# Reciprocal row sums sent to DRAM as single words, without transposes, and their factor of one half moved into v

## The chip, the core and the metric

The kernel runs on one core of a Trainium2 chip. The core has a matrix engine (TensorE, PE in the profile), a vector engine (VectorE, DVE), an engine for functions and copies (ScalarE, ACT), a general one (GpSimd, POOL) and SyncE (SP), which here only issues DMA transfers. DMAs are also issued from the queues of ACT and POOL. The metric is the time of one execution on the device in microseconds (us); the times before are a median of 3 executions, and a separate execution was profiled.

## The reference

One decoder block over 512 tokens of width 1024, all in float32. The input is normalised and goes through one wide projection. From that come two attention branches of 8 heads of width 64 each: the first (fox) has a forget bias in its logits, the second (moba) works on blocks of keys, which for 512 tokens and blocks of 256 comes to causal attention. Each branch is multiplied by a SiLU gate and projected; the two are merged with sigmoid gates, projected once more and added to the input. What the change touches is this part of it:

```
p = softmax(logits)                       # exp / row sum
y = (p @ v) * silu(z)                     # per head, then heads side by side
```

The softmax divides by the sum over keys, one number for each head and query. The kernel computes SiLU as z * (1 + tanh(z / 2)) * 0.5, so a factor of one half goes in somewhere.

## The kernel before, in words

Matmuls of full float32 accuracy are made of three products of rounded parts: each operand is split into a high part and the rest (`hi`, `lo`), so nearly every operand passes ACT (a copy, which rounds) and DVE (a subtraction) before PE reads it.

Attention runs as four groups of four heads: fox a, fox b, moba a, moba b (`plan`). In a group the heads are taken in two pairs (`pr` 0 and 1). For a head:

- `Tr` transposes q and k of a pair.
- `Aa` computes, for four blocks of 128 queries, the logits (L571, L572), the mask and the negated maximum on DVE (L574), and the exponential on ACT (L576), which also sums each row into `rs`. Queries lie on the partitions, so the sums of a head are a column of 128 numbers for each of the 4 blocks. After the second head of a pair `inverse_sums` takes the reciprocal of the pair's 2 x 4 columns on DVE (L591) into `ri`.
- `Bb` transposes the exponentials (L616), splits them (L622, L623) and multiplies them with v (L626, L627). v is held as its high part and the rest side by side (`evac_v`, L351 on ACT and L352 on DVE), so that the result has both in two halves of the partitions, which L651 and L652 add into `ypair`. The result is transposed: the 64 columns of a head lie on partitions, the 512 queries along them.
- `Yp` multiplies `ypair` by the SiLU gate (`ZS`, made in `unit_z` with no factor of one half) and the reciprocal sums, and splits the product (L677 to L680).

For `Yp` the reciprocals must lie along the queries and be the same on all 64 partitions of a head. For seven of the eight pairs this goes through DRAM:

- `sums_out` transposes the 128 x 8 reciprocals on PE into 8 x 128 (L596), copies them out of PSUM on ACT times 0.5 (L598) and stores them from ACT's queue as 8 rows of 512 bytes into `R_dram` (L599).
- `sums_in` reads each head's 2 KB back onto 64 partitions, two broadcast loads from ACT's queue (L606), into `rinv_bc`, which has one buffer. These can be issued only when the store has landed.
- `Yp` multiplies the broadcast with the gate on POOL (L677), and the result with `ypair` on DVE (L678).

For the last pair (moba b, pair 1) nothing goes through DRAM. `Yp` spreads the reciprocals times 0.5 over 64 columns a head on POOL (L670), transposes the four 128 x 128 blocks of that on PE (L673) into a bank of PSUM, and multiplies the gate with it on DVE (L674).

Between the steps of the attention groups stand units of other work ("filler"): the projections of later groups, gate projections and the first branch projection. A projection unit (`unit`) takes one of two PSUM banks (`pj`), does 24 matmuls and is copied out by ACT or DVE. After the attention come the merge gates (`GA`, `GB`), the moba branch projection (`wm`, L695 to L697), which reads what `Yp` made, and the output projection. The last `Yp` is called three units into the first gate products.

The functions are traced in a written order, and a planner at build time then sets the order of each engine's instructions, by its own durations, among those whose inputs and buffers are ready. An engine carries out its instructions in that order, the DMA issues of its queue among them: an issue that waits for an earlier transfer holds up what is queued behind it on the same engine. Transposes and projections share three PSUM banks (`tp`).

Of the kernel before, what the change touches and what calls it, by code (L numbers as in the profile page):

```python
# [29 lines left out]
def fox_moba_kernel(ctx: ExitStack, tc, xT, x, w_in, w_fl, w_fox, w_moba, w_out, cst, rope, out):  # L30
# [28 lines left out]
    def tp(name):  # L59
        return pst("tp", 3, name)  # L60
# [285 lines left out]
    def evac_v(p, name, t):  # L346
# [4 lines left out]
        A.activation(v[:, t, :, 0:HD], pv, AF.Copy)  # L351
        V.tensor_tensor(out=v[:, t, :, HD:P], in0=pv, in1=v[:, t, :, 0:HD].bitcast(F32), op=OP.subtract)  # L352
# [163 lines left out]
    def attn_group(br, half, gq, gk):  # L516
# [72 lines left out]
        def inverse_sums(pr):  # L589
            h0 = hb + 2 * pr  # L590
            V.reciprocal(ri[:, h0:h0 + 2, :], rs[:, h0:h0 + 2, :])  # L591

        def sums_out(pr):
            h0 = hb + 2 * pr
            p = tp("p_ri")
            T.transpose(p[:8, :P], ri[:, h0:h0 + 2, :].rearrange("p h t -> p (h t)"), ident)  # L596
            rt = sb.tile([8, P], F32, name="rinv_t", tag="rinv_t", bufs=1)
            A.activation(rt, p[:8, :P], AF.Copy, scale=0.5)  # L598
            A.dma_start(out=R_dram[h0:h0 + 2].rearrange("h t p -> (h t) p"), in_=rt)  # L599

        def sums_in(pr):
            if last and pr:
                return
            rb = st["r", pr] = stage["pool"].tile([P, S], F32, name="rinv_bc", tag="rinv_bc", bufs=1)
# [4 lines left out]
        def Bb(h):  # L609
            def go():  # L610
# [42 lines left out]
                if o == 0 and not (last and pr):  # L653
                    sums_out(pr)
                elif pr:
                    sums_in(1)
            return go

        def Yp(pr):
            def go():  # L660
# [4 lines left out]
                if last and pr:  # L665
                    zr, rb = ZS[br, gp], pst("lg", 2, "p_rinv")
                    h0 = hb + 2 * pr
                    rw = t2("u", 4, "rinv_w")
                    for o in range(2):
                        G.tensor_scalar(rw.rearrange("p (t o d) -> p t o d", o=2, d=HD)[:, :, o, :],  # L670
                                        ri[:, h0 + o, :, None].to_broadcast([P, NT, HD]), 0.5, None, op0=OP.mult)
                    for t in range(NT):
                        T.transpose(rb[:, t * P:(t + 1) * P], rw[:, t * P:(t + 1) * P], ident)  # L673
                    V.tensor_tensor(out=zr, in0=zr, in1=rb, op=OP.mult)  # L674
                else:
                    zr = st["r", pr]
                    G.tensor_tensor(out=zr, in0=ZS[br, gp], in1=zr, op=OP.mult)  # L677
# [558 lines left out]
```

## Time and profile before

| What | us |
|---|---|
| Median of 3 executions | 425.06 |
| Lowest and highest of them | 424.13, 425.23 |
| The profiled execution | 424.43 |
| Its span, first to last instruction | 422.5 |
| PE busy | 417.3 |
| VectorE (DVE) busy | 327.5 |
| ScalarE (ACT) busy | 279.7 |
| GpSimd (POOL) busy | 102.4 |

A row of the profile names the line of the kernel, the engine, the operation, what is written and read, and the shape, then how often (x) and how long. L596 is line 596. An engine's name with a q behind it (ACTq) is its queue: DMA issues and waits on semaphores, which aren't counted as busy time. PEld is the loading of weights into the array, which runs beside the matmuls. Matmuls overlap in the array, so one that lasts 0.27 us can take up less of PE's time; the chain of work in order of time shows what each adds to the path. "idle before <-releaser" behind a row is how long its engine stood idle before it and what ended that. The span is some 2 us shorter than the time of the same execution.

### The profile page before, as it was taken

To read this page: it belongs to the slowest core of one execution; us is meant where nothing else is said; L and a number is where in the kernel's file an instruction comes from. 1 tells how busy PE (TensorE), PEld (TensorE's weight loads), DVE (VectorE), ACT (ScalarE), POOL (GpSimd) and SP (SyncE) were. 2 spreads that over 40 slices of the span, in tenths; PEclk is the share of its full clock that TensorE was granted. 3 is DMA by queue.
4 is the path that set the end of the run, shared out by engine and by line. 5 is a ranking of instruction groups with operands and counts; after the bars stand their busy time and mean duration, and the time that the engine had idled before them with its cause. 6 is when DMAs were issued, how large, how long until landed. Compare 5 with 4: busy or idle time off the path is not lost.

```text
span 422.5 us, 7680 instructions
## 1 busy us (share of the span) xinstructions
PE 417.3 (99%) x2912; PEld 388.0 (92%) x2912; DVE 327.5 (78%) x575; ACT 279.7 (66%) x528; POOL 102.4 (24%) x120
## 2 busy tenths in 40 slices
PE   8999999999999999999999999999999999999996
PEld 6998899999999998899998888899999989988885
DVE  4669968799968779668666778767979698689883
ACT  5987327877877978569758687756655535686450
POOL 1067600224235550025650100340000000022230
PEclk9999999999999999999999999999999999999999
DMA  7982325567252123303122311673142603697494
GB/s 227 396 290 98 99 101 159 158 192 223 63 168 102 45 83 101 102 24 101 33 93 78 102 47 27 240 247 110 35 169 67 233 2 117 213 249 119 99 138 162
DMA packets 24484, 56.10 MB, mean 133 GB/s; under 512 B 2824, under 2 KB 7616, under 8 KB 24448
## 3 DMA queue, kind: packets, MB, share of 16 engines
q1 hardware_dynamic: 13536, 38.11, 28.0%
q0 software_dynamic: 3392, 8.39, 9.0%
q10 hardware_dynamic: 7520, 9.11, 6.8%
q8 instruction: 23, 0.38, 0.4%
q14 instruction: 13, 0.11, 0.1%
HBM read 48.11 MB, written 6.32 MB: 129 GB/s over the span
## 4 chain that ended last, share of the span: by engine, by line
PE 97%; DMA 1%; SPq 0%; DVE 0%; issue 0%
PE pb_GB L769 3%; PE pb_GA L769 3%; PE pb_GA L766 3%; PE pb_GB L766 3%; PE pb_GB L768 3%; PE pb_GA L768 3%; PE po L957 3%; PE po L956 3%; PE po L955 3%; PE pv L627 2%; PE lg L572 2%; PE pv L626 2%; PE lg L571 2%; PE pf L696 2%; PE pm L697 2%; PE pf L697 2%
## 5 line engine op out<-in xcount | busy, mean ns | idle before, releaser
L342 POOL TENSOR_TENSOR ff<-ss,mh 128x8 f32<-128x8 f32 x16 | 29.7, 1857 | 72.7 <-DVE ss L340 54.2
L576 ACT ACTIVATE p<-p,negm 128x128 f32<-128x128 f32 (+1 forms) x64 | 35.7, 558 | 13.0 <-DVE negm L574 12.0
L574 DVE CUSTOM_DVE_ANT_0 p<-lg,mask 128x128 f32<-128x128 f32 (+1 forms) x64 | 30.7, 485 | 15.0 <-PE lg L572 14.5
L904 POOL DMA_DIRECT2D wr_o<-in_w_out_dram x4 | 4.9, 1293 | 95.5 <-ACT wr_o L903 95.5
L142 DVE TENSOR_TENSOR wl_GA<-wr_ga,wh_GA 128x1024 fp32r<-128x1024 f32 x14 | 16.9, 1222 | 5.9 <-ACT wh_GA L140 3.9
L140 ACT ACTIVATE wh_GA<-wr_ga 128x1024 fp32r<-128x1024 f32 x14 | 14.6, 1059 | 10.1 <-PE pb_GA L768 5.1
L140 ACT ACTIVATE wh_GB<-wr_gb 128x1024 fp32r<-128x1024 f32 x14 | 14.6, 1059 | 9.5 <-PE pm L696 3.5
L571 PE MATMUL lg<-KH,QS 128*128 128x128 f32 (+1 forms) x64 | 20.4, 328 | 0.0
L918 DVE TENSOR_TENSOR wl_o<-wr_o,wh_o 128x1024 fp32r<-128x1024 f32 x14 | 17.0, 1219 | 3.8 <-ACT wh_o L917 3.8
L917 ACT ACTIVATE wh_o<-wr_o 128x1024 fp32r<-128x1024 f32 x14 | 14.8, 1060 | 7.6 <-PE pb_GB L768 2.8
L142 DVE TENSOR_TENSOR wl_GB<-wr_gb,wh_GB 128x1024 fp32r<-128x1024 f32 x14 | 16.9, 1221 | 3.5 <-ACT wh_GB L140 3.5
L652 DVE TENSOR_TENSOR ypair<-pv,ysh 64x512 f32<-64x512 f32 x16 | 11.0, 687 | 6.2 <-ACT ysh L651 5.8
L546 DVE SCALAR_TENSOR_TENSOR KL<-p_kT,cs,KH 64x512 fp32r<-64x512 f32 x16 | 12.0, 747 | 3.4 <-ACT KH L543 3.2
L623 DVE TENSOR_TENSOR ptl<-p_a,pth 128x512 fp32r<-128x512 f32 x16 | 10.9, 684 | 4.3 <-ACT pth L622 4.2
L651 ACT ACTIVATE ysh<-pv 64x512 f32<-64x512 f32 x16 | 9.5, 593 | 7.1 <-PE pv L627 4.7
L336 DVE TENSOR_REDUCE ss<-sq 128x8 f32<-128x512 f32 x16 | 10.8, 680 | 3.6 <-ACT sq L335 3.6
L766 PE MATMUL pb_GA<-Gh,wh_GA 128*128 128x256 f32 x48 | 13.5, 282 | 0.0
L768 PE MATMUL pb_GA<-Gl,wh_GA 128*128 128x256 f32 x48 | 13.5, 281 | 0.0
L769 PE MATMUL pb_GA<-Gh,wl_GA 128*128 128x256 f32 x48 | 13.5, 281 | 0.0
L769 PE MATMUL pb_GB<-Gh,wl_GB 128*128 128x256 f32 x48 | 13.5, 281 | 0.0
L768 PE MATMUL pb_GB<-Gl,wh_GB 128*128 128x256 f32 x48 | 13.4, 281 | 0.0
L766 PE MATMUL pb_GB<-Gh,wh_GB 128*128 128x256 f32 x48 | 13.3, 281 | 0.0
(461 smaller groups left out, 1794.1 us busy)
## 6 DMA issues: line engine op xcount, KB each, us to landing
wr_ga<-in_w_in_dram SPq DMA_DIRECT2D x8, 512.0 KB
wr_gb<-in_w_in_dram SPq DMA_DIRECT2D x8, 512.0 KB
wr_o<-in_w_out_dram SPq DMA_DIRECT2D x8, 512.0 KB
xt<-in_xT_dram SPq DMA_DIRECT2D x8, 256.0 KB
x<-in_x_dram SPq DMA_DIRECT2D x8, 256.0 KB
s_dramh<-sum_sh ACTq DMA_DIRECT2D x8, 256.0 KB
s_draml<-sum_sl ACTq DMA_DIRECT2D x8, 256.0 KB
wr_wf<-in_w_fox_dram SPq DMA_DIRECT2D x4, 512.0 KB
```

Source lines behind the costliest of these rows:

```text
L140: A.activation(hi[:, :, 0:n], src, AF.Copy)
L142: eng.tensor_tensor(out=lo[:, q, 0:n], in0=src[:, q], in1=hi[:, q, 0:n].bitcast(F32), op=OP.subtract)
L342: G.tensor_tensor(out=f2, in0=ss.rearrange("p t h -> p (t h)"), in1=mh, op=OP.pow)
L571: T.matmul(lg[:, :n], qs[:, qt], kh[:, :n], start=True, stop=False)
L574: V.tensor_tensor_reduce(pt, lg[:, :n], mask[:, 512 - n:512], -0.125, 3.0e38, op0=OP.add, op1=OP.min, accum_out=mkn[:, hh, i:i + 1])
L576: A.activation(pt, pt, AF.Exp, bias=mkn[:, hh, i:i + 1], scale=-1.0, accum_out=rs[:, hh, i:i + 1])
L697: T.matmul(p, lo[:, k, cc], yh, start=False, stop=(k == 3))
L766: T.matmul(o, hi[:, k, cc], lh, start=(n < 3 and c == 0 and k == 0), stop=False, skip_group_check=True)
L768: T.matmul(o, hi[:, k, cc], ll, start=False, stop=False, skip_group_check=True)
L769: T.matmul(o, lo[:, k, cc], lh, start=False, stop=(k == 3), skip_group_check=True)
L917: A.activation(wide(hi), wide(R[key, c]), AF.Copy)
L918: V.tensor_tensor(out=wide(lo), in0=wide(R[key, c]), in1=wide(hi).bitcast(F32), op=OP.subtract)
```

## The change

Three things change.

The reciprocals are stored from where they lie. `sums_out` has no transpose and no copy any more: one DMA reads the 128 x 8 numbers of a pair from `ri` and writes them to `R_dram` in the same order as before. There the numbers of one partition lie 128 words apart.

The factor of one half goes from the copy (L598, and L670 for the last pair) to v: the ACT copy of v's high part is scaled by 0.5, and the DVE subtraction becomes a multiplication by 0.5 and a subtraction in one instruction.

The last pair goes through DRAM like the others: a store after its first head, two broadcast loads after its second, and the gate product on POOL. Its `rinv_bc` takes one of the four buffers of the tag "u", which outlives the attention stage, because its `Yp` runs in the next one.

```diff
-        A.activation(v[:, t, :, 0:HD], pv, AF.Copy)
-        V.tensor_tensor(out=v[:, t, :, HD:P], in0=pv, in1=v[:, t, :, 0:HD].bitcast(F32), op=OP.subtract)
+        A.activation(v[:, t, :, 0:HD], pv, AF.Copy, scale=0.5)
+        V.scalar_tensor_tensor(v[:, t, :, HD:P], pv, 0.5, v[:, t, :, 0:HD].bitcast(F32), op0=OP.mult, op1=OP.subtract)
...
         def inverse_sums(pr):
-            h0 = hb + 2 * pr
-            V.reciprocal(ri[:, h0:h0 + 2, :], rs[:, h0:h0 + 2, :])
+            h = slice(hb + 2 * pr, hb + 2 * pr + 2)
+            V.reciprocal(ri[:, h, :], rs[:, h, :])
 
         def sums_out(pr):
-            h0 = hb + 2 * pr
-            p = tp("p_ri")
-            T.transpose(p[:8, :P], ri[:, h0:h0 + 2, :].rearrange("p h t -> p (h t)"), ident)
-            rt = sb.tile([8, P], F32, name="rinv_t", tag="rinv_t", bufs=1)
-            A.activation(rt, p[:8, :P], AF.Copy, scale=0.5)
-            A.dma_start(out=R_dram[h0:h0 + 2].rearrange("h t p -> (h t) p"), in_=rt)
+            h = slice(hb + 2 * pr, hb + 2 * pr + 2)
+            A.dma_start(out=R_dram[h].rearrange("h t p -> p h t"), in_=ri[:, h, :])
 
         def sums_in(pr):
-            if last and pr:
-                return
-            rb = st["r", pr] = stage["pool"].tile([P, S], F32, name="rinv_bc", tag="rinv_bc", bufs=1)
+            rb = st["r", pr] = (t2("u", 4, "rinv_bc") if last and pr else
+                                stage["pool"].tile([P, S], F32, name="rinv_bc", tag="rinv_bc", bufs=1))
...
-                if o == 0 and not (last and pr):
+                if o == 0:
                     sums_out(pr)
                 elif pr:
                     sums_in(1)
...
-                if last and pr:
-                    zr, rb = ZS[br, gp], pst("lg", 2, "p_rinv")
-                    h0 = hb + 2 * pr
-                    rw = t2("u", 4, "rinv_w")
-                    for o in range(2):
-                        G.tensor_scalar(rw.rearrange("p (t o d) -> p t o d", o=2, d=HD)[:, :, o, :],
-                                        ri[:, h0 + o, :, None].to_broadcast([P, NT, HD]), 0.5, None, op0=OP.mult)
-                    for t in range(NT):
-                        T.transpose(rb[:, t * P:(t + 1) * P], rw[:, t * P:(t + 1) * P], ident)
-                    V.tensor_tensor(out=zr, in0=zr, in1=rb, op=OP.mult)
-                else:
-                    zr = st["r", pr]
-                    G.tensor_tensor(out=zr, in0=ZS[br, gp], in1=zr, op=OP.mult)
+                zr = st["r", pr]
+                G.tensor_tensor(out=zr, in0=ZS[br, gp], in1=zr, op=OP.mult)
                 V.tensor_tensor(out=y, in0=y, in1=zr, op=OP.mult)
```

## The prediction, made before the result was known

> **What bounds the kernel now.** I read the page first: busy time by engine, granted clock, the chain of work that ended last.
>
> ```profile
> PE 417.3 (99%) x2912; PEld 388.0 (92%) x2912; DVE 327.5 (78%) x575; ACT 279.7 (66%) x528; POOL 102.4 (24%) x120
> PEclk9999999999999999999999999999999999999999
> PE 97%; DMA 1%; SPq 0%; DVE 0%; issue 0%
> ```
>
> The chain is TensorE from one end to the other, at full granted clock. An average can hide a stage in which PE waits, so next the busy time of the stretches that the change touches, the four attention groups and the first gate products (columns: PE, PEld, DVE, ACT, POOL, clock, DMA share, GB/s):
>
> ```profile
> 65.00:110.00 45.00, 45.00 (x370) 44.31 (x369) 40.31 (x90) 34.35 (x79) 12.42 (x9) 1.00 0.57 173
> 205.00:250.00 45.00, 45.00 (x295) 40.83 (x294) 31.96 (x67) 31.74 (x67) 12.47 (x14) 1.00 0.25 80
> 250.00:284.00 34.00, 34.00 (x211) 30.19 (x210) 25.90 (x46) 24.38 (x49) 8.42 (x11) 1.00 0.46 152
> 284.00:345.00 61.00, 61.00 (x485) 59.57 (x484) 50.21 (x50) 35.41 (x50) 0.00 (x0) 1.00 0.35 111
> ```
>
> PE is busy for the whole of each. So here time comes off only where PE work comes off, and it is added only where some other engine makes PE wait. Everything below is asked in those two ways.
>
> **The PE work that goes.** The chain in order of time gives each matmul its own share of the path (start, us on the path):
>
> ```profile
> 91.38 0.11 PE p_ri L596
> ...
> 256.07 0.11 PE p_ri L596
> ...
> 288.24 0.44 PE p_rinv L673 x4
> ```
> ```profile
> L596 PE MATMUL p_ri<-ident,rinv x7: 270/271/272, 91.2 to 255.9; 128*8 128x128 f32 x7
> ...
> L673 PE MATMUL p_rinv<-ident,rinv_w x4: 270/272/273, 288.1 to 288.4; 128*128 128x128 f32 x4
> ```
>
> The two p_ri rows are the first and the last of the seven. A transpose lasts 0.27 us, but they overlap in the array, and on the path each takes 0.11. The change removes 7 x 0.11 = 0.77 us and the four of the last pair, 0.44 us: together 1.21 us. Nothing is put on PE in their place.
>
> **What goes from the other engines.** ACT loses seven copies of the small result, DVE one product with PSUM, POOL the two spreads of the last pair; POOL gets an eighth gate product instead (1.29 us, the last shape of the second fence):
>
> ```profile
> L598 ACT ACTIVATE rinv_t<-p_ri x7: 247/266/267, 91.6 to 256.6; 8x128 f32<-8x128 f32 x7
> ...
> L674 DVE TENSOR_TENSOR zs_mzb<-zs_mzb,p_rinv x1: 686/686/686, 288.7 to 288.7; 128x512 f32<-128x512 f32 x1
> ...
> L670 POOL TENSOR_SCALAR rinv_w<-rinv x2: 837/1343/1849, 280.0 to 281.8; 128x256 f32<-128x256 f32 x2
> ```
> ```profile
> L677 POOL TENSOR_TENSOR rinv_bc<-zs_mzb,rinv_bc x1: 1294/1294/1294, 263.1 to 263.1; 128x512 f32<-128x512 f32 x1
> ```
>
> That is 1.9 us of ACT, 0.7 of DVE and 1.4 of POOL, all beside a full PE: worth nothing by itself. Banks of PSUM come free too, worth nothing while PE never waits.
>
> **The half in v.** The 16 copies of v get a constant factor and the 16 subtractions become a multiply and subtract in one. The nearest rows are the same two operations on the q and k halves, with and without a factor:
>
> ```profile
> L539 DVE SCALAR_TENSOR_TENSOR QS<-p_qT,cs,QS x16: 744/750/759, 67.6 to 249.9; 64x512 fp32r<-64x512 f32 x16
> ...
> L652 DVE TENSOR_TENSOR ypair<-pv,ysh x16: 673/689/697, 96.5 to 281.1; 64x512 f32<-64x512 f32 x16
> ```
> ```profile
> L538 ACT ACTIVATE QS<-p_qT,cs x16: 669/682/687, 66.5 to 249.2; 64x512 fp32r<-64x512 f32 x16
> ...
> L651 ACT ACTIVATE ysh<-pv x16: 589/592/602, 95.4 to 280.2; 64x512 f32<-64x512 f32 x16
> ```
>
> At most 61 ns more on DVE and 90 on ACT, so 16 x 0.061 = 1.0 us and 16 x 0.090 = 1.4 us at the top; at the bottom nothing, or a few ns less. The rows differ by a per-partition factor, here it is a constant, so I take the lower half. What waits for these is the PSUM bank of the next projection unit, and the windows show PE full with what ACT and DVE do now. Cost on the path zero; were the cover gone, 0.15 us for each of 16 units, 2.4 us.
>
> **The store, which is the unknown.** It now moves 2 heads x 4 blocks x 128 words straight from where the reciprocal lies. In DRAM neighbouring words of a partition are 128 words apart, so 8 rows of 512 bytes become 1024 words of 4 bytes. The store is issued from ACT's queue, and the two broadcast loads that read it back are issued there as well; they wait for it to land, and with them all ACT work queued behind. This is how it stands at the last of the seven round trips and at the one with the longest distance:
>
> ```profile
> 256.60 0.25 ACT L598 ACTIVATE rinv_t<-p_ri 8x128 f32<-8x128 f32 x1
> 256.88 0.27 ACTq L599 DMA_DIRECT2D r_dram<-rinv_t  x1
> 257.20 1.06 ACT L140 ACTIVATE wh_GA<-wr_ga 128x1024 fp32r<-128x1024 f32 x1 [0.35 <-DVE wr_ga L730]
> 258.14 0.45 ACTq L606 DMA_DIRECT2D rinv_bc<-r_dram  x1
> ...
> 230.91 0.27 ACTq L599 DMA_DIRECT2D r_dram<-rinv_t  x1
> ...
> 233.81 1.11 ACTq L606 DMA_DIRECT2D rinv_bc<-r_dram  x2
> 234.97 0.60 ACT L651 ACTIVATE ysh<-pv 64x512 f32<-64x512 f32 x1 [2.19 <-PE p_b L616]
> ```
> ```profile
> L606 ACTq EVENT_SEMAPHORE  x11: 17/38/1266, 93.5 to 257.3; - x11
> ```
>
> From store to first load is 1.26 and 2.90 us, middle 2.1; the 8-row store can land within 1.26. ACT's queue already waits up to 1266 ns ahead of a load, and ACT has stood idle 2.19 us, while the window 205 to 250 shows PE at 45.00 of 45.00. So an ACT stand of about 2.2 us is covered.
>
> How much later do 1024 words land? No row has a packet of that size, so bounds from the queues:
>
> ```profile
> q1 hardware_dynamic: 13536, 38.11, 28.0%
> ...
> q10 hardware_dynamic: 7520, 9.11, 6.8%
> ```
>
> Spread over 16 engines it is 64 packets each. Upper end: each costs as much as ACT's queue's average packet, 0.068 x 16 x 422.5 us / 7520 = 61 ns, for 1211 bytes; 64 x 61 ns = 3.9 us. Lower end: the other queue's packet is 0.28 x 16 x 422.5 / 13536 = 140 ns for 2815 bytes; the line through both is 49 ns per 1000 bytes and 2 ns at no bytes, so 64 x 2 ns = 0.1 us. I take 1 us: time goes with bytes in these rows, but they hold few small writes. The store then lands within about 1.3 + 1 = 2.3 us and the loads wait 0 to 1 us more than now, which the 2.2 us cover. Cost on the path: zero.
>
> The Trainium skill, "DMA: Bandwidth & Descriptors", section "Rules for kernel authors", speaks against this store: a non-contiguous last dimension becomes one descriptor per element, and one should rearrange so that it is contiguous; its "Specifications" add that writes under 512 B are done as read-modify-write. No run so far shows such a write. The same page's measured table ("Bandwidth") has loads of 64 small packets at about 10.5 ns a packet; as an estimate by that page 64 would be 0.7 us, and the sum would be the same as with my 1 us.
>
> Against lateness stands that the store no longer waits for its turn on PE. The reciprocal is there well before:
>
> ```profile
> 249.31 0.18 DVE L591 RECIPROCAL rinv<-rsum 128x8 f32<-128x8 f32 x1
> ```
>
> It ends at 249.5 and the transpose of it came at 256.07, the store at 256.88. The store may now be issued up to 7 us earlier, wherever the planner finds ACT's queue free.
>
> **The eighth round trip** is new: one store and two loads, 0.27 + 2 x 0.46 = 1.2 us of ACT's queue (the fence above), less than the 1.9 us of copies removed. Behind its wait on ACT stand copies for the gate products; the same 2.2 us cover holds. On POOL the product waits for the broadcast, and the page has POOL empty from 284 to 345. Its result is first read by the moba projection:
>
> ```profile
> L695 PE MATMUL pm<-yhm,wh_wm x32: 388/392/403, 331.7 to 383.6; 128*128 128x512 f32 x32
> ```
>
> That is some 40 us after it is made today (about 291), so even a round trip of 10 us is hidden. SP's queue gets nothing new.
>
> **Sum.** Against the profiled execution (424.43 us, of which 422.5 are span): 424.43 - 1.21 = 423.2. The median shown is 425.06, the profiled one lies 0.63 below it. The four executions (424.13, 424.43, 425.06, 425.23) have a mean of 424.71, and I set the change against that: 424.71 - 1.21 = 423.5 us, 0.37% under the median. About 0.3% (1.28 us, so 423.78 to 426.34) is what a measurement of this kernel can tell from no change, so a good part of this case falls inside it.
>
> **Rivals.**
> - *The words land late and ACT holds up PE* (slower). Place: ACT's queue at each load of the sums. With the upper end, 3.9 us, the store lands 5.2 us after its issue, ACT stands 5.2 - 2.1 = 3.1 us, 0.9 more than is covered, eight times: 7.2 us, so 430.7 us. It decides from 3.0 us of lateness on (1.3 + 3.0 - 2.1 = 2.2); each 0.1 us more costs 0.8. At 3.5 us it is 4.0, 427.5 us. For it: one ordered queue, and a wait of 1.27 us there already. Against it: the two queues' times go with bytes, and the store can go out earlier. The skill's rule on one descriptor per element names this danger; by the rows here it is the less likely.
> - *The gain doesn't arrive*: the place of a transpose is taken by a wait of PE for what came beside it, or the planner, which sets another order, leaves small gaps. Then 1.21 us come back as idle time and it stays at 424.7 us. For it: ACT and DVE gain up to 2.4 us of work in the v units. Against it: the chain has PE on 97%, with no engine close behind.
>
> **How the numbers follow.** The forecast, nothing new on PE's path: 0.60; its own range is 424.13 - 1.21 = 422.9 to 425.23 - 1.21 = 424.0, with a few tenths for small gaps. Most of it, 0.44, lies below 423.78, 0.16 above. Late words: 0.26, of which 0.24 slower beyond 0.3% and 0.02 within. Gain not arriving: 0.14, of which 0.12 within and 0.02 slower. Faster 0.44, same 0.30, slower 0.26. The range goes from 422.6 (0.3 below the forecast's own) to 428.0, about half of the late words: it leaves out some 0.02 below and 0.13 above.
>
> **What would show it.** Right: no p_ri and p_rinv row, PE still full from 25 to 381 us, matmuls 11 fewer, eight stores and sixteen loads, the v subtraction at 0.41 to 0.48 us, the store issued soon after the reciprocal, the wait ahead of the loads under 2.2 us. Wrong: an ACT wait on the sums of 3 us or more with PE idle beside it, a store whose issue is itself long (now 0.27 us), the DMA share rising around the stores, or PE gaps in another stage, which would mean the planner's order and not the words.

## The result and the profile after

The changed kernel takes 491.88 us (median of 6 executions, 481.71 to 494.21), the kernel before 424.69 us beside it (6 executions, 424.13 to 425.23). Between the least disturbed executions of the two (481.71 and 484.08 us for the changed kernel) the ratio is 1.137, with a 95% interval of 1.135 to 1.139, or 58 us; the profiled execution of the changed kernel, from which the account below is taken, is one of the longer ones with 491.16 us and a span of 489.5 us, so its single figures are good to some 3%. Between the medians the ratio is 1.158. The range of the prediction ended at 428.0.

Busy time by engine, PE in 40 slices, the granted clock, ACT's DMA queue and the chain of the changed kernel:

```profile
PE 434.4 (89%) x2901; PEld 401.9 (82%) x2901; DVE 327.5 (67%) x574; ACT 277.8 (57%) x521; POOL 103.3 (21%) x119
PE   8999999949699599498698699499689999999997
PEclk9999999979899889799599799799979999999999
...
q10 hardware_dynamic: 15888, 9.38, 9.0%
...
PE 62%; DMA 18%; issue 7%; DVE 5%; ACT 3%; POOL 2%; ACTq 2%; SPq 0%; DVEq 0%; POOLq 0%
DMA r_dram<-rinv 14%; DMA rinv_bc<-r_dram 3%; PE pb_GB L753 3%; PE pb_GB L750 3%; PE pb_GB L752 3%; PE po L941 3%; PE po L940 3%; PE po L939 3%; PE pb_GA L750 2%; PE pb_GA L752 2%; PE pb_GA L753 2%; ACTq L601 2%; PE pm L681 2%; PE pm L680 2%; PE pm L679 2%
```

TensorE had the chain to itself before (97%); now 14% of it, 0.141 of 489.5 = 69 us, is the store of the reciprocals. PE's row, which should read 9 throughout, has holes, and behind most of them the clock has one too. The waits of PE in the changed kernel (who waits, for whom, us in all, times, longest):

```profile
PE pj_fvb L314 <- ACT qn_fkb L321: 8.0, 1, 8.0
PE p_cc L611 <- DVE KL L546: 7.1, 1, 7.1
PE pj_mkb L314 <- ACT qn_mqb L321: 6.6, 1, 6.6
PE pv L621 <- ACT pth L617: 6.4, 1, 6.4
PE pz_mzb L413 <- DVE v_mvb L352: 6.0, 1, 6.0
PE pj_mva L314 <- ACT qn_mka L321: 5.9, 1, 5.9
PE pb_GA L750 <- ACT wh_GA L140: 5.5, 1, 5.5
PE lg L571 <- ACT KH L543: 4.3, 1, 4.3
```

Eight waits, one for each round trip, 49.8 us together. None of the releasers has anything to do with the reciprocals: they are copies of a projection, of keys, of exponentials, of gate weights. Why they came late is seen on ACT's own timeline, at one of the round trips (start, duration; brackets: idle before):

```profile
222.87 0.36 ACTq L595 DMA_DIRECT2D r_dram<-rinv  x1
...
225.39 1.06 ACT L140 ACTIVATE wh_mvb<-wr_mvb 128x1024 fp32r<-128x1024 f32 x1
233.81 1.10 ACTq L601 DMA_DIRECT2D rinv_bc<-r_dram  x2
234.96 0.68 ACT L541 ACTIVATE KH<-p_kT,cs 64x512 fp32r<-64x512 f32 x1 [8.51 <-issue]
```
```profile
L601 ACTq EVENT_SEMAPHORE  x13: 17/38/10442, 92.6 to 338.6; - x13
```

The store is issued at 222.87. ACT goes on with other work for 3.6 us, and then its queue stands until 233.81, because the loads wait for the store to land. The first load goes out 10.9 us after the store; over the eight round trips the two are 9.4 to 13.0 us apart, 11.5 in the mean. The longest wait ahead of a load is now 10442 ns, where it was 1266.

Seven of the gaps come about in this way. The eighth (pb_GA, 350.9 to 356.4) comes later than ACT's stand and by another way: the broadcast of the last pair, issued at 343.07, lets POOL go on only at 352.77, and the products that wait for it one after the other stand ahead of the next gate weights in DVE's and ACT's order:

```profile
352.77 1.26 POOL L661 TENSOR_TENSOR rinv_bc<-zs_mzb,rinv_bc 128x512 f32<-128x512 f32 x1 [14.37 <-DMA rinv_bc<-r_dram]
...
354.06 0.69 DVE L662 TENSOR_TENSOR ypair<-ypair,rinv_bc 128x512 f32<-128x512 f32 x1 [6.98 <-POOL rinv_bc L661]
...
354.78 0.63 ACT L663 ACTIVATE yhm<-ypair 128x512 fp32r<-128x512 f32 x1 [7.53 <-DVE ypair L662]
```

One of the prediction's windows, as it looks now (PE, PEld, DVE, ACT, POOL, clock, DMA share, GB/s):

```profile
205.00:250.00 45.00, 38.31 (x272) 36.97 (x273) 26.77 (x58) 27.60 (x61) 12.36 (x15) 0.85 0.19 53
```

PE is no longer full, and while it is busy it does less: in 45 us from 205 it is busy for 38.31 us and does 272 matmuls, where it did 295. The stretch after one gap, in steps of 2 us, shows the second loss:

```profile
228.00:230.00 2.00, 2.00 (x20) 1.99 (x18) 0.00 (x0) 0.00 (x0) 0.03 (x1) 1.00 0.00 0
...
234.00:236.00 2.00, 0.00 (x0) 0.00 (x0) 0.00 (x0) 1.03 (x2) 0.00 (x0) 0.50 0.45 96
...
240.00:242.00 2.00, 2.00 (x10) 1.90 (x10) 1.96 (x8) 0.99 (x4) 0.27 (x1) 0.50 0.78 262
242.00:244.00 2.00, 2.00 (x15) 1.92 (x14) 0.00 (x0) 0.38 (x1) 1.88 (x2) 0.90 0.03 8
244.00:246.00 2.00, 2.00 (x17) 1.86 (x17) 1.41 (x5) 1.37 (x4) 1.84 (x5) 1.00 0.00 0
```

PE stands for the 6.6 us of the list above, from about 230.2 to 236.8, the granted clock falls to 0.50, and it stays there until about 242.4, with PE busy again: 10 matmuls in 2 us, where 17 to 20 go through at full clock.

So the 67.0 us of longer span (489.5 - 422.5) split in two. PE's idle time grew from 422.5 - 417.3 = 5.2 to 489.5 - 434.4 = 55.1 us: 49.9 us, the eight waits. PE's busy time grew from 417.3 to 434.4 although 1.2 us of work was gone: 18.3 us. Nearly all of that is the clock: PE's busy time in each slice of 1 us, times the part of the clock that was not granted in it, adds up to 16.9 us.

### The profile page after: what moved, and what is told of

Same layout as the page of the kernel before. It is cut to its first block, busy times and chain, and to the rows that moved or that the text cites. A ratio compares the mean times of both kernels' runs of the same rounds, so it can differ in the third digit from the quotient of the medians.

```text
span 489.5 us, 7673 instructions
## 1 busy us (share of the span) xinstructions
PE 434.4 (89%) x2901; PEld 401.9 (82%) x2901; DVE 327.5 (67%) x574; ACT 277.8 (57%) x521; POOL 103.3 (21%) x119
## 3 DMA queue, kind: packets, MB, share of 16 engines
q10 hardware_dynamic: 15888, 9.38, 9.0%
## 4 chain that ended last, share of the span: by engine, by line
PE 62%; DMA 18%; issue 7%; DVE 5%; ACT 3%; POOL 2%; ACTq 2%; SPq 0%; DVEq 0%; POOLq 0%
DMA r_dram<-rinv 14%; DMA rinv_bc<-r_dram 3%; PE pb_GB L753 3%; PE pb_GB L750 3%; PE pb_GB L752 3%; PE po L941 3%; PE po L940 3%; PE po L939 3%; PE pb_GA L750 2%; PE pb_GA L752 2%; PE pb_GA L753 2%; ACTq L601 2%; PE pm L681 2%; PE pm L680 2%; PE pm L679 2%
## 5 line engine op out<-in xcount | busy, mean ns | idle before, releaser
L541 ACT ACTIVATE KH<-p_kT,cs 64x512 fp32r<-64x512 f32 x16 | 10.8, 678 | 27.9 <-issue 27.7
L142 DVE TENSOR_TENSOR wl_GA<-wr_ga,wh_GA 128x1024 fp32r<-128x1024 f32 x14 | 16.9, 1222 | 5.0 <-ACT wh_GA L140 5.0
L142 DVE TENSOR_TENSOR wl_GB<-wr_gb,wh_GB 128x1024 fp32r<-128x1024 f32 x14 | 16.9, 1223 | 3.5 <-ACT wh_GB L140 3.5
L618 DVE TENSOR_TENSOR ptl<-p_b,pth 128x512 fp32r<-128x512 f32 x16 | 10.9, 683 | 10.2 <-ACT pth L617 10.1
L314 PE MATMUL pj_fvb<-wh_fvb,Gh 128*128 128x256 f32 x32 | 10.0, 312 | 8.0 <-ACT qn_fkb L321 8.0
L617 ACT ACTIVATE pth<-p_b 128x512 fp32r<-128x512 f32 x16 | 9.5, 595 | 12.8 <-issue 10.2
L571 PEld LDWEIGHTS lg<-KH,QS 128*128 128x128 f32 x64 | 12.2, 191 | 5.1 <-ACT KH L543 4.5
L314 PE MATMUL pj_mkb<-wh_mkb,Gh 128*128 128x256 f32 x32 | 10.5, 327 | 6.6 <-ACT qn_mqb L321 6.6
L314 PE MATMUL pj_mva<-wh_mva,Gh 128*128 128x256 f32 x32 | 10.0, 313 | 5.9 <-ACT qn_mka L321 5.9
```

The source lines that it names most:

```text
L142: eng.tensor_tensor(out=lo[:, q, 0:n], in0=src[:, q], in1=hi[:, q, 0:n].bitcast(F32), op=OP.subtract)
L314: T.matmul(p[:, :n], Gh[:, kk, st], hi[:, k, :n], start=(kk == 0), stop=False)
L571: T.matmul(lg[:, :n], qs[:, qt], kh[:, :n], start=True, stop=False)
```

## The experiments

The theory after the result: a store of 1024 words takes some 11 us to land; the loads that wait for it stand in ACT's one queue, and PE soon runs out of what ACT makes. Rivals: another part of the change costs the time; the queue or the planner's order is at fault and not the landing; and, for the landing itself, that it is a price per packet.

### One part at a time

`v_half` keeps the transposes and the last pair as before, and does only the half in v. `rows8` has the whole change but for the words: transposed rows, for all eight pairs.

```diff
 # rows8, sums_out, against the changed kernel
-            A.dma_start(out=R_dram[h].rearrange("h t p -> p h t"), in_=ri[:, h, :])
+            p = tp("p_ri")
+            T.transpose(p[:8, :P], ri[:, h, :].rearrange("p h t -> p (h t)"), ident)
+            rt = sb.tile([8, P], F32, name="rinv_t", tag="rinv_t", bufs=1)
+            A.activation(rt, p[:8, :P], AF.Copy)
+            A.dma_start(out=R_dram[h].rearrange("h t p -> (h t) p"), in_=rt)
```

> The kernel before with the half of the gate in v alone; the sums go out in rows through the transposes as before. Theory 1 (the words land some 11 us after their issue, ACT's queue stands at the loads, PE runs dry): this part costs nothing on the path, 424 to 426 us, PE full from 25 to 381 us. Theory 2 (the v units or the planner's new order of all engines lose the time): a large part of the 58 us is here, 440 us or more.

> The changed kernel, but the sums are transposed and copied and stored as 8 rows of 512 bytes again, now for all eight pairs; the half stays in v and the last pair goes through DRAM. Theory 1: 424 to 427 us (PE has 0.11 us more and 0.44 less than in the kernel before), the loads follow their store by 1.3 to 3 us. Theory 3 (the eighth round trip through DRAM, late in the attention, is what costs): 430 us or more, with PE idle around the last pair.

Measured: v_half 424.58 us (424.20 to 425.01), 1.0001 of before (0.9991 to 1.0010). rows8 424.04 us (423.66 to 425.40), 0.9990 (0.9981 to 0.9999). The half in v costs nothing, and an eighth round trip costs nothing: rows8 takes 0.5 us less than the 424.55 us beside it, where four transposes fewer and one more are worth 0.33. In neither does PE's list of waits have one behind the first 10 us. What is left of the change is the shape of the store. The wait ahead of the loads in rows8:

```profile
L605 ACTq EVENT_SEMAPHORE  x11: 17/38/1357, 93.5 to 257.3; - x11
```

`after_again` is the changed kernel unaltered, once more.

> The changed kernel itself once more, for a profile beside the others on one chip. Every theory: 481 to 494 us, the loads 11 to 12 us behind their stores, eight gaps of PE.

It took 491.92 and 496.60 us, the second above the range that was expected. In its trace PE has ten waits of 2.5 us and more, not eight, 52.3 us together.

### The landing, or what stands behind it

Three kernels keep the 1024 words and change who waits for them. `words_sp` issues the loads from SP's queue and `words_pool` from POOL's:

```diff
             for o in range(2):
-                A.dma_start(out=rb[o * HD:(o + 1) * HD, :],
+                nc.sync.dma_start(out=rb[o * HD:(o + 1) * HD, :],      # words_pool: G.dma_start
```

> The changed kernel with the two broadcast loads issued from SP's queue in place of ACT's; the word stores stay as they are. Theory 1: the store still lands 11 to 12 us after its issue, but ACT no longer stands, PE stays full, 423 to 430 us; what is left over 423.5 is weight loads held up on SP's queue. Theory 4 (1024 single words keep the DMA engines or the DRAM busy so that everything else is late): still above 470 us.

> The changed kernel with the two broadcast loads issued from POOL's queue, where the product that needs them waits anyway. Theory 1: 423 to 432 us, PE full apart from places where the q and k norms on POOL come late. Theory 4: still above 470 us.

Measured: words_sp 443.64 us (442.74 to 444.41), ratio 1.0453 (1.0436 to 1.0471); words_pool 450.44 us (449.68 to 451.10), 1.0607 (1.0591 to 1.0623). The largest waits of PE, first words_sp, then words_pool, and what POOL itself waited for in words_pool:

```profile
PE p_kT L531 <- POOL qn_mka L380: 4.8, 1, 4.8
PE pb_GA L750 <- ACT wh_GA L140: 4.2, 1, 4.2
PE lg L571 <- DMA KH<-KH: 2.6, 1, 2.6
```
```profile
PE pb_GA L752 <- DMA S0l<-s_draml: 9.7, 1, 9.7
PE p_kT L531 <- POOL qn_fkb L344: 5.5, 1, 5.5
```
```profile
POOL rinv_bc L601 <- DMA r_dram<-rinv: 114.6, 8, 33.2
```

Store and load are still 8.6 to 12.1 us apart in words_sp. With ACT free of the wait some 39 and 32 of the 58 us are gone. Most of the waits that are left are the same wait on other engines. In words_sp the gate product on POOL, which needs the loads, stands ahead of work on the keys of the next group (4.8 us), and the last product on DVE, which stands 8.1 us for POOL's, ahead of gate weights (4.2 us); why the DMA of keys came late (2.6 us) isn't shown. In words_pool the loads too stand in POOL's order, ahead of a transfer (S0l, 9.7 us) and of work on keys (5.5 us). Both expectations, at most 430 and 432 us, were missed: POOL's order too has things behind the loads that PE needs within 10 us.

`words_behind` leaves the loads on ACT but puts them later in its order, behind all that ACT has been given by then, and moves the gate product behind the next head's logits, the last one by six units.

```diff
-                elif h:
-                    sums_in(0)
...
-                elif pr:
-                    sums_in(1)
+                else:
+                    with behind(mybir.EngineType.Activation):
+                        sums_in(pr)
...
-        return ([Tr(0)], [Aa(0), Aa(1), Tr(1), Bb(0), Aa(2), Bb(1), Yp(0), Aa(3)], [Bb(2), Bb(3)], [Yp(1)])
+        return ([Tr(0)], [Aa(0), Aa(1), Tr(1), Bb(0), Aa(2), Bb(1), Aa(3), Yp(0)], [Bb(2), Bb(3)], [Yp(1)])
...
-        if n == 2:
+        if n == 8:
             gate[0]()
```

> The changed kernel with the word stores as they are and the loads still on ACT's queue, but each pair of loads tied behind the last ACT copy of the pair's second head, the product of the first pair after the fourth head's softmax, and the last product six units later. Theory 1 (the time goes where ACT's queue stands for a landing): ACT does its own work in the 11 us, most of the 58 us comes back, 424 to 440 us, while the words land as late as ever. If the late landing itself or the eight slow writes cost time beside ACT: still above 460 us.

Measured: 443.74 us (443.10 to 444.38), 1.0453 (1.0434 to 1.0472), 3.7 us above the range that was expected. Now 17 to 24 us lie between store and load. At the first seven round trips ACT no longer stands at the loads. At the last one it does, though the row of the waits, whose longest is 38 ns, doesn't show it: the store lands 19.9 us after its issue, and ACT is idle for 15.0 us. The row of the waits, the store in the chain in order of time, ACT's next instruction behind the loads, and what is left of PE's waits:

```profile
L599 ACTq EVENT_SEMAPHORE  x13: 17/38/38, 111.2 to 276.1; - x13
```
```profile
281.88 19.86 DMA r_dram<-rinv
```
```profile
302.91 0.60 ACT L759 ACTIVATE e_GA<-pb_GA 128x512 f32<-128x512 f32 x1 [15.03 <-issue]
```
```profile
PE pb_GA L749 <- ACT e_GA L759: 4.1, 1, 4.1
PE pb_GA L751 <- DMA S0l<-s_draml: 3.9, 1, 3.9
PE pv L619 <- DVE ypair L645: 2.8, 1, 2.8
```

The same store as in the changed kernel, and some 39 of the 58 us are back once ACT's queue doesn't have to wait for seven of the eight landings. Of the three waits that are left, e_GA is the instruction in front of which ACT stood for the eighth, and S0l is a load of 512 KB on POOL's queue, issued 0.16 us before the last store. The third stands behind another store from ACT's queue (s_draml, for which L276 waits 3.9 us) that was issued 2 to 3 us behind a store of words.

So the words also hold up transfers beside them. The clearest case is in the changed kernel, where the loads of 512 KB follow one another as in the kernel before: the last of the eight, in the kernel before, in spaced (below), whose words lie 64 bytes apart, and in the changed kernel, the last number being the us from issue to landing:

```profile
S3l<-s_draml POOLq DMA_DIRECT2D x1, 512.0 KB, 6.1
```
```profile
S3l<-s_draml POOLq DMA_DIRECT2D x1, 512.0 KB, 6.5
```
```profile
S3l<-s_draml POOLq DMA_DIRECT2D x1, 512.0 KB, 14.3
```

In the kernel before all eight take 4.0 to 6.4 us. In the changed kernel the three that were issued between the last store and its landing take 10.7 to 14.3. In words_behind the seven from 281.7 us on take 12.4 to 21.5, but there they are issued in quicker succession as well. The theory that the words keep everything else late explains too little to be the whole loss, but it has a part in what is left.

### What makes the store land late

All kernels of this part store from where the reciprocals lie, from ACT's queue; they change how many pieces there are and where in DRAM they go. In these kernels the reader gets half of the reciprocals, mostly ones, or the right ones in another order, so they serve for times alone, and each ran once. The edits, each against the changed kernel's `[16, NT, P]` and its store:

```diff
 # half_words: one head of the two, read for both
+            A.dma_start(out=R_dram[h0:h0 + 1].rearrange("h t p -> p h t"), in_=ri[:, h0:h0 + 1, :])
 # spaced: words 64 bytes apart (apart32: 8 in place of 16; apart8: 2); filled with ones at the start
+    R_dram = dr.tile([16, NT, P, 16], F32, name="r_dram")
+            A.dma_start(out=R_dram[h][:, :, :, 0].rearrange("h t p -> p h t"), in_=ri[:, h, :])
 # rows_apart: neighbouring words as before, the eight rows of a pair 16 KB apart; filled likewise
+    R_dram = dr.tile([16, NT, 4096], F32, name="r_dram")
+            A.dma_start(out=R_dram[h][:, :, 0:P].rearrange("h t p -> p h t"), in_=ri[:, h, :])
 # row32B: the 8 words of a partition side by side
+    R_dram = dr.tile([8, P, 8], F32, name="r_dram")
+            A.dma_start(out=R_dram[hb // 2 + pr].rearrange("p (h t) -> p h t", t=NT), in_=ri[:, h, :])
```

> The changed kernel with each store cut to the first head of its pair: 512 words in place of 1024, and both loads read that head (the second head's reciprocals are left out, so half of the attention output is scaled by the wrong sums). Store to first load now 11 to 12 us. If each word has its price in DRAM: about 6 us from store to load, and the whole loses some 10 to 20 us instead of 58. If any write of such small pieces has a fixed price: still 11 us and 480 us.

> The changed kernel with as many words, but each 64 bytes from the next one in DRAM instead of 4 (the room is filled with ones before the attention; the loads read 2 KB of it, so the reciprocals that arrive are mostly ones and the output is wrong by them). If words that are neighbours in DRAM hold each other up: 2 to 4 us from store to load and 424 to 428 us. If each word has its price wherever it lies: still 11 us and 480 us.

> The changed kernel with the eight numbers of a partition stored as they lie, 128 rows of 32 bytes, the same 4 KB in one contiguous piece of DRAM; the loads read them in that order, so the reciprocals arrive at the wrong queries. By price per piece: 128 in place of 1024, 11 us comes down to 2 to 3 us, 423 to 426 us. By a fixed price for pieces under 512 bytes: still 11 us and 480 us.

> As the run with words 64 bytes apart, but 32 bytes apart, two words in each 64 bytes (ones fill the room, the loads read 2 KB of it, so the reciprocals that arrive are mostly ones). If two neighbours in 64 bytes cost little more than one: store to load as with 64 bytes, 2.6 to 3.5 us, near 438 us. If the price goes up with each pair of neighbours: 4 us or more.

> As the runs with words 64 and 32 bytes apart, but 8 bytes apart, eight words in each 64 bytes and 8 KB for a store (ones fill the room, the loads read 2 KB of it, so the reciprocals that arrive are mostly ones). If the price follows the number of neighbours in 64 bytes (2 cost nothing more, 16 cost some 8 us): 5 to 7 us from store to load, 445 to 460 us. If only dense words pay: 3 us and 438 us.

> The changed kernel with the words of a row neighbours as before (128 words in 512 bytes), but the eight rows of a store 16 KB apart in place of 512 bytes (the loads read 2 KB of which the first 512 bytes are a row and the rest ones, so the reciprocals that arrive are wrong). If near neighbours hold each other up: still 9 to 12 us from store to load and above 470 us. If it is the crowding of 1024 pieces into one 4 KB stretch of DRAM: well under that, 3 to 6 us.

The distance from store to first load is the landing time wherever ACT's queue stood waiting in between. Read that way:

| Kernel | Pieces of a store | Pieces that share 64 bytes | Store to first load, us | Time, us |
|---|---|---|---|---|
| rows8 | 8 of 512 B | 1 | 1.3 to 1.5 at the shortest | 424.04 |
| row32B | 128 of 32 B | 2 | 1.4 to 2.1 at the shortest | 423.07 |
| row16B (below) | 256 of 16 B | 4 | 1.6 to 2.9 at the shortest | 425.45 |
| spaced | 1024 of 4 B | 1 | 2.6 to 2.9 | 438.32 |
| apart32 | 1024 of 4 B | 2 | 2.8 to 2.95 | 437.55 |
| apart8 | 1024 of 4 B | 8 | 4.3 to 4.6 | 432.05 |
| half_words | 512 of 4 B | 16 | 8.7 to 13.0 | 480.07 |
| changed kernel | 1024 of 4 B | 16 | 9.4 to 13.0 | 491.88 |
| rows_apart | 1024 of 4 B, rows 16 KB apart | 16 | 20.8 to 34.5 | 623.88 |

Two timelines of ACT side by side, spaced and rows_apart, at the same round trip:

```profile
227.88 0.37 ACTq L597 DMA_DIRECT2D r_dram<-rinv  x1
...
230.77 1.10 ACTq L603 DMA_DIRECT2D rinv_bc<-r_dram  x2
```
```profile
346.10 0.37 ACTq L597 DMA_DIRECT2D r_dram<-rinv  x1
...
371.02 1.10 ACTq L603 DMA_DIRECT2D rinv_bc<-r_dram  x2
372.17 0.38 ACT L351 ACTIVATE v_mvb<-pj_mvb 128x256 fp32r<-128x256 f32 x1 [24.78 <-issue]
```

And the waits ahead of the loads in half_words and apart8 (shortest, median, longest in ns):

```profile
L602 ACTq EVENT_SEMAPHORE  x13: 17/38/8310, 92.3 to 329.8; - x13
```
```profile
L603 ACTq EVENT_SEMAPHORE  x12: 17/38/3728, 92.2 to 283.8; - x12
```

It is not a price per word: half as many words land hardly sooner. Nor is it a fixed price of any small write: 1024 words that lie 32 or 64 bytes apart land within 2.95 us. What the slow ones have in common is that words from many partitions are neighbours in DRAM: with 8 of them in 64 bytes it is 4.4 us, with 16 it is 9 and more. That the rows of a pair lie within 4 KB isn't the cause, since moving them 16 KB apart made it two to three times as long, and why it did is open. For apart8 and for rows_apart the landing lies outside what either branch of the expectation named, so the runs give an order of the cases and no formula. The Trainium skill, "DMA: Bandwidth & Descriptors", "Specifications", says that writes under 512 B are done as read-modify-write. Neighbours that have to wait for one another would look like this, but 1024 such writes without near neighbours took 2.9 us, so the rule alone doesn't give the time. The stores of ones are not what makes the landing early in spaced: rows_apart has them too and lands latest. No run shows the mechanism in the memory; they show only what the time depends on.

The times of spaced, apart32 and apart8 say less than their landing, and spaced missed its 424 to 428 us: each has gaps elsewhere (in spaced 2.7 us at a DMA of keys ahead of the first store, 2.4 us, and 2.7 us behind the last product, as in the eighth gap of the changed kernel), and the stores of ones that fill their larger tables, 512, 256 and 64 KB, were not tried apart from the rest.

row32B is the change with an early landing, but with the numbers in another order at the reader. PE is full there from 65 to 381 us, and its span is 421.4 against 422.5 us of the profile before, 1.1 less:

```profile
65.00:381.00 316.00, 315.97 (x2312) 299.07 (x2311) 250.77 (x436) 221.92 (x424) 68.68 (x79) 1.00 0.39 121
```

### Versions that might keep the gain

The first way to larger pieces is DVE's transpose of 32 x 32 blocks: 8 rows of 32 words for each 32 partitions, four stores of 8 rows of 128 bytes.

```diff
+    r32 = con.tile([P, 32], F32, name="r32")
+    G.memset(r32, 1.0)
...
-            V.reciprocal(ri[:, h, :], rs[:, h, :])
+            V.reciprocal(r32[:, 0:8].rearrange("p (h t) -> p h t", t=NT), rs[:, h, :])
+            tt = st["t", pr] = sb.tile([P, 32], F32, name="rinv_t", tag="rinv_t", bufs=2)
+            V.transpose(tt, r32)
...
-            A.dma_start(out=R_dram[h].rearrange("h t p -> p h t"), in_=ri[:, h, :])
+            for b in range(4):
+                A.dma_start(out=R_dram[h].rearrange("h t p -> (h t) p")[:, 32 * b:32 * b + 32], in_=st["t", pr][32 * b:32 * b + 8, :])
```

> The changed kernel, but VectorE transposes the reciprocals in blocks of 32 x 32, and they go out in four stores of 8 rows of 128 bytes: no PE transposes and no words. By price per piece 8 pieces a store: landing about as the rows of before, 1.5 to 3 us; ACT has three more issues of 0.27 us a pair. 422.8 to 424.5 us, that is the 1.2 us of PE that the change was to bring. By a fixed price for pieces under 512 bytes: 480 us.

Measured: 430.82 us (429.85 to 431.82), 1.0139 (1.0119 to 1.0159). That is above the range that was expected. The words land in time, no load waits more than 38 ns and ACT has no stand at one, but one gap of PE is left, in the last pair. The DMA share while its broadcast is under way, the product on POOL, and DVE and ACT behind it:

```profile
281.40:289.80 8.40, 8.36 (x71) 8.15 (x69) 2.06 (x3) 2.10 (x3) 0.00 (x1) 1.00 0.70 210
```
```profile
289.80 1.25 POOL L666 TENSOR_TENSOR rinv_bc<-zs_mzb,rinv_bc 128x512 f32<-128x512 f32 x1 [8.80 <-DMA rinv_bc<-r_dram]
```
```profile
291.09 0.69 DVE L667 TENSOR_TENSOR ypair<-ypair,rinv_bc 128x512 f32<-128x512 f32 x1 [6.11 <-POOL rinv_bc L666]
291.70 1.22 DVE L142 TENSOR_TENSOR wl_GA<-wr_ga,wh_GA 128x1024 fp32r<-128x1024 f32 x1
```
```profile
291.81 0.63 ACT L668 ACTIVATE yhm<-ypair 128x512 fp32r<-128x512 f32 x1 [6.65 <-DVE ypair L667]
...
293.30 0.58 ACT L765 ACTIVATE e_GA<-pb_GA 128x512 f32<-128x512 f32 x1
```

The broadcast is issued at 281.38 and has landed only at 289.8, with the DMA engines busy at 0.70; the product on DVE stands ahead of the rest of the gate weights in DVE's order, and the copy of its result ahead of gate weights and of the emptying of a PSUM bank (e_GA) in ACT's. PE waits for that bank: 4.2 us, and more by the clock. Three kernels go after this gap: `blk32_late` traces that last product six units later (n == 8 in place of 2), `blk32_7` gives the last pair back to PE as it was before, and `blk32_tied` ties the last product behind what DVE and ACT have been given by then:

```diff
+                with ExitStack() as tied:
+                    if last and pr:
+                        tied.enter_context(behind())
+                        tied.enter_context(behind(mybir.EngineType.Activation))
+                    V.tensor_tensor(out=y, in0=y, in1=zr, op=OP.mult)
...
-        if n == 2:
+        if n == 8:
             gate[0]()
```

> The kernel with 32 x 32 transposes on VectorE and rows of 128 bytes, with the last product six units of gate work later, so that VectorE no longer stands in front of the parts that PE needs when the last broadcast lands 8 us after its issue. Theory 1: the 4.3 us gap at 294 us and the lower clock behind it go, PE full, 1.2 us less PE work than before: 423 to 424 us. If the four more issues on ACT cost: 425 us or more.

> The same 32 x 32 transposes and rows of 128 bytes for the first seven pairs, the last pair spread and transposed on PE as in the kernel before, the half in v. Theory 1: 0.77 us of PE work less and no late broadcast at the end, 423.5 to 424.3 us.

> The kernel with 32 x 32 transposes on VectorE and rows of 128 bytes, the last product traced six units later and now also tied behind the gate work of those units on VectorE and ACT, which the planner had pulled forward again in the run before. If the 4 us gap at 290 us comes from the last product standing in front of the gate's parts: the gap goes, PE is full, 423 to 424 us. If it comes from elsewhere: 429 us or more.

Measured: blk32_late 431.10 us (1.0144, 1.0125 to 1.0163), blk32_7 425.46 us (1.0020, 1.0011 to 1.0029), blk32_tied 424.88 us (1.0006, 0.9997 to 1.0015). To trace the product later did nothing: the planner took it forward to the same place. Tied, the gap is gone. All three expectations, 423 to 424.3 us, were missed. One wait is in the lists of both of the others, a projection unit whose bank comes free late:

```profile
PE pj_fvb L314 <- DVE v_fvb L352: 0.8, 1, 0.8
```

In blk32_tied this and 0.7 us more than before at the kernel's start make up the 1.5 us that are missing (1.21 us of work gone, 0.30 us slower). In blk32_7 it is half of the 1.65 us that are missing (0.77 gone, 0.88 slower); the rest isn't traced.

The second way keeps a partition's words together in DRAM and lets the reader sort them: 256 pieces of 16 bytes, and the products read the broadcast in permuted order. `row16B_tied` adds the tie.

```diff
-    R_dram = dr.tile([16, NT, P], F32, name="r_dram")
+    R_dram = dr.tile([16, P, NT], F32, name="r_dram")
...
+            A.dma_start(out=R_dram[h].rearrange("h p t -> p h t"), in_=ri[:, h, :])
...
+                zr = st["r", pr].rearrange("r (p t) -> r t p", t=NT)
+                G.tensor_tensor(out=zr, in0=ZS[br, gp].rearrange("r (t p) -> r t p", t=NT), in1=zr, op=OP.mult)
+                V.tensor_tensor(out=y.rearrange("r (t p) -> r t p", t=NT), in0=y.rearrange("r (t p) -> r t p", t=NT), in1=zr, op=OP.mult)
```

> The changed kernel with DRAM ordered by head, partition, block: 256 rows of 16 bytes a store, four of them neighbours in 64 bytes. The loads bring each head's 2 KB as it lies, and POOL's and VectorE's products read and write it in the permuted order, so the whole block is computed. If neighbours within 64 bytes hold each other up at the rate of the words (16 neighbours, 9 us late): 4 neighbours, about 2 us late, landing 3 to 4 us, ACT's stand mostly covered, 423 to 424.5 us, the 1.2 us of PE kept. If any partial write beside another costs the whole 9 us: 480 us.

> The kernel with rows of 16 bytes, with the last product placed and tied in the same way. Its last gaps of 0.8 us go: 423 to 424.5 us. Without effect: as the run before, 424.2 to 428.2 us.

Measured: row16B 425.45 us (424.22 to 428.24), 1.0021 (1.0005 to 1.0037), above what was expected; row16B_tied 423.94 us (423.62 to 424.46, 11 executions), 0.9986 (0.9977 to 0.9995) of the 424.58 us of the kernel before beside it. Leaving aside row32B, whose reader gets the words in another order, it has the lowest median here, 0.14% below the kernel before. That is less than the 0.3% by which a comparison like the first one can be told from no change; the interval over these many executions excludes 1. But rows8, which keeps the transposes, is at 0.9990 (0.9981 to 0.9999), and the two intervals overlap: that leaving the transposes out is worth anything is not shown by the times. From 65 to 381 us PE is as good as full:

```profile
65.00:381.00 316.00, 315.89 (x2311) 298.74 (x2310) 253.80 (x434) 221.46 (x424) 70.60 (x79) 1.00 0.38 121
```

Of the 1.2 us of PE work that went about half arrives (424.58 - 423.94 = 0.64 us). The other half is lost at the start of the kernel, where PE waits 0.8 and 0.5 us for its first operands, 0.8 us more than before; why it does isn't shown.

## Why the prediction was wrong

The step that failed is the term "The store, which is the unknown". It bounded the lateness of 1024 words at 0.1 to 3.9 us and took 1 us; it was some 10 us (11.5 us from store to load in the mean, less the 1.3 us of the store with rows). Its bounds came from the time that packets take on the queues. That figure was not even bad: the changed kernel's queue has 15888 - 7520 = 8368 packets more and spends 0.090 x 16 x 489.5 - 0.068 x 16 x 422.5 = 245 us more on them, 29 ns each, between the two ends of 2 and 61 ns. Sixty-four of those are 1.9 us. But the waiter doesn't wait for the packets to have been handled, it waits for the store to have landed, and that came 9 to 13 us after its issue. A row with a landing in it stood in the profile (the wait ahead of the loads), but only for rows of 512 bytes, and no row had words that are neighbours in DRAM. The upper end should have been called open.

The Trainium skill's rule against this store ("DMA: Bandwidth & Descriptors", "Rules for kernel authors", one descriptor per element) agrees with the trace: eight stores of 1024 words, and 8368 packets more on the queue. The estimate from that page's figure for a packet, 0.7 us, failed for the same reason as the one from the rows.

The rival of the late words had the mechanism, ACT's queue standing at the loads, and its sum comes near. apart8, whose words are 3.0 to 3.3 us later than rows, has at the first seven round trips no wait of PE above 0.6 us, so the point at which the rival decides, 3.0 us, fits. With the 11.5 us that were measured, its sum gives 11.5 - 2.1 - 2.2 = 7.2 us for each round trip, eight times 57.6; PE's idle time grew by 49.9. That is so close in part by luck. The 2.1 us of ACT's work were the old order's; in the new one ACT goes on for 1.3 to 7.9 us behind the store. The 2.2 us of cover came from a stand of ACT that PE itself had ended ("[2.19 <-PE p_b L616]"), which doesn't show that PE can do without ACT for so long; at the first seven round trips ACT stood 5.4 to 9.7 us, and PE's gaps were from nothing to 3.7 us shorter. What the rival had not got is the clock after a gap, nearly all of 18.3 us.

Point by point for the rest:

- The PE work that goes, 1.21 us: right. The changed kernel has 2912 - 2901 = 11 matmuls fewer, and row32B, where the store lands early, has a span 1.1 us shorter and takes 423.07 us against 424.55 beside it.
- The half in v costs nothing on the path: right (v_half, 1.0001). The subtraction was to take 0.41 to 0.48 us; the medians of its four groups are 0.418 to 0.425 us, where they were 0.410 to 0.424.
- The eighth round trip is hidden: right for rows8, wrong for the changed kernel, where it is the eighth gap, 5.5 us. There and in blk32_4st its product, waiting for the broadcast, stood in DVE's order ahead of gate weights. The prediction named the copies behind the loads on ACT, and asked when the product's result is read, but not what is queued behind the product on DVE.
- The store can go out earlier: right that it does (the reciprocal starts at 222.63 and the store at 222.87 in the round trip shown), wrong as an argument, since the loads go out earlier with it.
- What would show it: of the signs named for "wrong" one came, the ACT wait of 3 us and more with PE idle beside it. The store's issue was no longer than 0.38 us, and the DMA share around the stores did not rise: it is 0.00 in the window from 228 to 230, with the words under way. Here a transfer was late with the DMA engines idle by the profile.
- "The gain doesn't arrive" happened in part, in row16B and two of the blk32 kernels: a wait of 0.8 us at a projection unit (blk32_tied, blk32_7), and waits of up to 1.3 us in all at the start, where the kernel before waits 0.5, ate what PE saved or part of it.

## What to carry to other kernels

Take the cost of a store from when its waiter is released, not from the packets' time on the queue, and look at where its pieces lie in DRAM: small pieces from many partitions that are neighbours there landed three times later and more than the same pieces spread out, or than four or eight words joined. When a layout must be turned on the way through DRAM, keep what one partition holds together in the write and let the reader's access pattern do the turning; here 16 bytes in place of 4 took the landing from 11 to under 3 us. And before a wait is put into an ordered queue, list what stands behind it on that engine and on each engine that uses the result, and add the clock that a gap of PE costs to the gap itself. To see whether an engine stood, look at its idle time before the next instruction and not only at the row of its waits: the 15 us of words_behind are in the one and not in the other.

## What the runs showed of the hardware

- 1024 words of 4 bytes landed 2.9 us after their issue when 32 or 64 bytes apart, 4.4 us when 8 bytes apart, 9.4 to 13.0 us side by side, and 20.8 to 34.5 us side by side with rows 16 KB apart. The last has no explanation here. In words_behind one store side by side, with seven loads of 512 KB beside it, took 19.9 us.
- Loads of 512 KB that were issued while a store of words side by side was under way landed 10.7 to 14.3 us after their issue (changed kernel), against 4.0 to 6.4 us in the kernel before and 3.9 to 6.5 us in spaced, whose words lie 64 bytes apart.
- After PE had stood for some 6 us the granted clock was 0.50, and it stayed so for about 5.6 us of renewed work. The Trainium skill, "TensorE: Matmul & The Clock Gate", "Part 1: The HAM clock gate", says that the gate knows half and full rate and opens after at least one busy window of about 3.4 us; the two rates agree with the trace, and its 5.6 us are longer than one such window. In the changed kernel the clock that was not granted while PE was busy comes to 16.9 us, a third of the 49.8 us of the gaps.
